# Head sums of an RWKV block: one fp32 product, or two fp32r products of a split operand

## The chip, the cores and the metric

The kernel runs on one core of a Trainium2 chip. The metric is the device time of one execution in microseconds (us); the median of several runs counts. A core has five engines that work in parallel, each with its own queue of instructions in fixed order: TensorE (in profiles PE, its weight loads PEld), VectorE (DVE), ScalarE (ACT), GpSimd (POOL) and SyncE (SP), which issues the transfers here. An instruction that needs another engine's result waits on a semaphore, and everything behind it in its queue waits with it.

## The reference

One residual block on x (1 x 1024 x 1024, float32): a norm, one large input projection, two branches side by side (stick-breaking attention with 8 heads of 64 channels, RWKV-7 time mixing with 8 heads of 64 channels), a gated merge with an output projection, and a SwiGLU feed-forward part. The change lies in the RWKV branch, cut here to what uses sums over a head's 64 channels:

```python
kk = (k * k_k).reshape(B, S, H, N)
kk = kk / jnp.maximum(jnp.linalg.norm(kk, axis=-1, keepdims=True), 1e-12)   # sum of squares over N
k = k * (1.0 + (a - 1.0) * k_a)
y = wkv7_scan(r_h, heads(decay), k_h, v_h, kk, heads(a))
mean = jnp.mean(y, axis=-1, keepdims=True)
var = jnp.mean(jnp.square(y - mean), axis=-1, keepdims=True)                # sum of squares over N
y = ((y - mean) * lax.rsqrt(var + GN_EPS)).reshape(B, S, RW_WIDTH) * lnx_w + lnx_b
bonus = (jnp.sum(r_h * k_h * r_k, axis=-1, keepdims=True) * v_h)            # sum over N
return ((y + bonus.reshape(B, S, RW_WIDTH)) * g)
```

## The kernel before

Activations lie with channels on the 128 partitions and tokens along the free axis. Two heads of 64 channels make a pair, and the RWKV branch has 4 pairs; each pair is worked in two halves of 512 tokens (`H`). One pair and one half is a unit, so there are 8 units. A sum over a head's channels is a sum over 64 partitions, made by TensorE: the left operand is `ones`, a 128 x 128 block matrix with a 64 x 64 block of ones for each head, and the right operand the 128 x 512 tile to be summed. The result has the sum on each of the head's 64 rows.

The large products run in fp32r, a form of fp32 that TensorE takes at another rate than plain fp32. To keep precision, an operand x is split into a high part (x cast to fp32r, on ScalarE) and a low part (x minus the high part, also fp32r, mostly on VectorE): the method `split`. Each k-step of a large product is then three fp32r products (high by high, high by low, low by high: `mm3`).

Work is recorded first and ordered afterwards. Each call such as `nc.tensor.matmul` becomes an `Op` with a price from the function `cost`, and `schedule` places the ops one by one on their engines by these prices, by priorities, and by when a tile's place comes free. Each engine then issues in that order, fixed when the kernel is built. So any new or cheaper operation can move others on all engines.

Stages, as the profile names them by tiles:

- `norm_in` and `lora`, up to some 90 us.
- The RWKV stage: `project` makes `k`, `r`, `v` of a pair (psum tiles `d`, rows `d_d<-big_h`), `rw_elementwise` prepares a unit, `rw_inverse` inverts small triangular blocks on VectorE (62 small dependent operations for a unit, tiles `q`, rows `q_q`), `rw_chain` carries the state through 8 chunks a unit (`c_c<-b_sv,b_nx`, then `c_c<-b_xv,b_bkt`; GpSimd scales the old state into `sp` meanwhile), and `rw_post` normalises. Gate projections (`gate_tiles`, also `d_d`) have a low priority and fill TensorE between.
- `attention`: per head products `e_e<-b_kst,...`, sigmoids on ScalarE (tile `nb`, behind a load of another table of functions, which waits for the last logarithm and exponential of `rw_post`), a scan on VectorE (`b_nb<-b_nb`), transposes (`c_c<-cst_cst,b_nb`), a split into `b_wt`, and products into `y`. The projections for the pairs to come (`d_d` again, with the splits `b_kst`, `b_ql`, `b_vhl`, `wlo`) run between.
- `merge`, `output`, `ffn`: large products.

Each unit makes three sums with `ones`: the squares of `k` (tile `t0` into `pn`, in front of everything that the inverse needs), `r * k * r_k` (tile `rk` into `pb`, for the bonus `bv`), and the squares of `y` in `rw_post` (tile `t0` into `pn`). That makes 24 products of 128 x 128 by 128 x 512 in plain fp32. SBUF tiles of class `b` share 27 places of 1040 columns; a plain fp32 tile of up to 520 columns takes half a place, other tiles a whole one.

Of the kernel before, what the change touches and what calls it, by code (L numbers as in the profile page):

```python
# [7 lines left out]
F32R = mybir.dt.float32r  # L8
BF16 = mybir.dt.bfloat16
AF = mybir.ActivationFunctionType  # L10
ALU = mybir.AluOpType
# [4 lines left out]
P = 128  # L16
# [3 lines left out]
H = 512  # L20
# [20 lines left out]
CC_ID, CC_CEN, CC_ONE, CC_MA, CC_DM, CC_TI, CC_SC, CC_N = 0, 128, 256, 384, 512, 640, 896, 1408  # L41
# [189 lines left out]
class Block:  # L231
# [325 lines left out]
    def proj(self, w, hf, cls="d"):  # L557
# [3 lines left out]
        self.mm3(ps, w, self.hT, KT, lambda x, k: x[:, k, :], lambda x, k: x[k // 4][:, k % 4, sl])  # L561
        return ps


    def rstd(self, srcs, junk):
        nc = self.nc
        ss = self.t("tiny", [P, 4])
        for i, s in enumerate(srcs):
            nc.scalar.activation(junk, s, AF.Square, accum_out=ss[:, i : i + 1])
        return self.rstd_of(ss, len(srcs))  # L570
# [20 lines left out]
def hybrid_block(tc, x, w_in, consts, params, rows, ups, gup, w_sb, w_rw, w_o, w_fg, w_fu, w_fd, out):  # L591
    b = Block(tc, {a.tensor.name for a in (x, w_in, consts, params, rows, ups, gup, w_sb, w_rw, w_o, w_fg, w_fu, w_fd)})
    nc = b
    T = b.t
    with ExitStack() as es:
        b.open(es)
        b.cls("cst", 1, CC_DM)
        b.cls("par", 1, PC_N)
        b.cls("small", 3, 16)
        b.cls("tiny", 4, 4)  # L600
        b.cls("ss", 8, 4)
        b.cls("carry", 5, 1)
        b.cls("pl", 3, 8)
        b.cls("bf", 2, P)
        b.cls("sp", 3, CH)
        b.cls("q", 4, 256)
        b.cls("big", 4, 4 * S)
        for n in ("raw", "whi", "wlo"):
            b.cls(n, 2, S)
        b.cls("b", NB, 1040, halves=True)  # L610
        for n, k in (("d", 2), ("e", 2), ("c", 2), ("y", 2)):
            b.cls(n, k, H, psum=True)

        cst, par = T("cst", [P, CC_DM]), T("par", [P, PC_N])
        b.xin = []
        for m in range(8):
            b.xin.append(T("b", [P, D], F32, "x"))
            nc.sync.dma_start(b.xin[m], x[m * P : m * P + P, :])
            if m == 0:
                nc.sync.dma_start(cst, consts[:, 0:CC_DM])  # L620
                b.gbc = T("b", [P, D])
                nc.sync.dma_start(b.gbc, rows[0:1, :].broadcast_to([P, D]))
            if m == 3:
                b.w_lora = [b.load(w_in[24], [P, KT, P])]
                nc.sync.dma_start(par, params)
            if m == 5:
                b.w_lora.append(b.load(w_in[25], [P, KT, P]))
        b.ident = cst[:, CC_ID : CC_ID + P]
        b.cen = cst[:, CC_CEN : CC_CEN + P]
        b.ones = cst[:, CC_ONE : CC_ONE + P]  # L630
        b.mask_a = cst[:, CC_MA : CC_MA + P]
        b.tinit = consts[:, CC_TI : CC_TI + 256]
        b.scanm = consts[:, CC_SC:CC_N]
        b.eps = T("small", [P, 2])
        nc.gpsimd.memset(b.eps[:, 0:1], RMS_EPS)
        nc.gpsimd.memset(b.eps[:, 1:2], GN_EPS)
        b.identb = T("bf", [P, P], BF16)
        nc.gpsimd.tensor_copy(b.identb, b.ident)
        b.dmask = T("bf", [P, P], BF16)
        dm = T("q", [P, P])  # L640
        nc.sync.dma_start(dm, consts[:, CC_DM : CC_DM + P])
        nc.gpsimd.tensor_copy(b.dmask, dm)
        b.om = T("small", [P, 14])
        nc.gpsimd.tensor_scalar(out=b.om, in0=par[:, PC_MU : PC_MU + 14], scalar1=-1.0, scalar2=1.0, op0=ALU.mult, op1=ALU.add)
        b.oka = T("small", [P, 4])
        nc.gpsimd.tensor_scalar(out=b.oka, in0=par[:, PC_KA : PC_KA + 4], scalar1=-1.0, scalar2=1.0, op0=ALU.mult, op1=ALU.add)
        b.pc = lambda col: par[:, col : col + 1]

        b.gsc = [b.scratch([P, S], f"gsc{j}") for j in range(16)]
        b.orw_d = [b.scratch([P, S], f"orw{p}") for p in range(PAIRS)]  # L650
        b.x2_d = b.scratch([S, D], "x2d")
        b.w_in, b.w_sb, b.w_rw = w_in, w_sb, w_rw
        b.ngate = 0

        b.steady = STEADY[0]
        norm_in(b)
        lora(b, ups, gup)
        b.steady = STEADY[1]
        rwkv(b)
        b.steady = STEADY[2]  # L660
        attention(b)
        b.steady = STEADY[3]
        merge(b)
        b.steady = True
        output(b, x, w_o, rows)
        ffn(b, w_fg, w_fu, w_fd, rows, out)
        b.issue()


def norm_in(b):  # L670
    nc = b.nc
    T = b.t
    b.hT = tuple([T("big", [P, 4, S], F32R, "h") for q in range(2)] for i in range(2))
    b.table("natural_log_exp_and_others")
    def scale(m):
        xs = T("b", [P, D], F32, "xs")
        return xs, b.rstd([b.xin[m]], xs)

    ahead = [scale(0), scale(1)]
    for m in range(8):  # L680
        xs, r = ahead.pop(0)
        nc.vector.scalar_tensor_tensor(out=xs, in0=b.xin[m], scalar=r, in1=b.gbc, op0=ALU.mult, op1=ALU.mult)
        if m + 2 < 8:
            ahead.append(scale(m + 2))
        b.to_channels(("e", "c"), xs, m, b.hT)
        if m in (2, 4):
            w = b.w_lora[m // 2 - 1]
            hi, lo = T("b", [P, KT, P], F32R), T("b", [P, KT, P], F32R)
            nc.scalar.copy(hi, w)
            nc.gpsimd.tensor_tensor(out=lo, in0=w, in1=hi, op=ALU.subtract)  # L690
            b.w_lora[m // 2 - 1] = hi, lo
# [91 lines left out]
def rwkv(b):  # L783
    T = b.t
    b.table("natural_log_exp_and_others")
    carry = {}
    units = [[{}, {}] for p in range(PAIRS)]

    def project(p):
        for name, j in (("k", 4 + p), ("r", p), ("v", 8 + p)):  # L790
            w = b.weights(b.w_in[12 + j], [P, KT, P])
            for hf in range(2):
                ps = b.proj(w, hf)
                units[p][hf][name] = T("b", [P, H], F32, name)
                shifted(b, ps, carry, j, hf, units[p][hf][name])

    project(0)
    for p in range(PAIRS):
        for hf in range(2):
            rw_elementwise(b, units[p][hf], p, hf, b.spill[p][hf])  # L800
        if p + 1 < PAIRS:
            with Offset(b, PROJ):
                project(p + 1)
        gate_tiles(b, GATES_R[p])
        with Offset(b, CHAIN):
            for hf in range(2):
                rw_chain(b, units[p], p, hf)
                with Offset(b, POST):
                    rw_post(b, units[p][hf], p, hf, b.spill[p][hf])


def rw_elementwise(b, u, p, hf, spill):
    nc = b.nc
    T = b.t
    pc, oka, cen, ones, mask_a, tinit = b.pc, b.oka, b.cen, b.ones, b.mask_a, b.tinit
    r, k, v = u["r"], u["k"], u["v"]
    lo, hi = slice(0, CH), slice(CH, P)
    halves = (lo, hi)
# [18 lines left out]

    t0 = T("b", [P, H], F32, "tmp")
    nc.scalar.activation(t0[:], k[:], AF.Square, scale=pc(PC_KK + p))
    pn = T("e", [P, H])  # L840
    nc.tensor.matmul(pn[:], lhsT=ones, rhs=t0[:], start=True, stop=True)
    rn = T("b", [P, H], F32, "tmp")
    nc.vector.tensor_scalar(out=rn[:], in0=pn[:], scalar1=1e-24, scalar2=None, op0=ALU.max)
    nc.scalar.activation(rn[:], rn[:], AF.Ln)
# [18 lines left out]

    rk = T("b", [P, H], F32, "tmp")
    nc.vector.scalar_tensor_tensor(out=rk[:], in0=r[:], scalar=pc(PC_RK + p), in1=kp[:], op0=ALU.mult, op1=ALU.mult)
    pb = T("e", [P, H])
    nc.tensor.matmul(pb[:], lhsT=ones, rhs=rk[:], start=True, stop=True)
    bv = T("b", [P, H], F32, "bv")
    nc.vector.tensor_tensor(out=bv[:], in0=v[:], in1=pb[:], op=ALU.mult)
    u["bv"] = bv  # L870
# [153 lines left out]
def rw_post(b, u, p, hf, spill):  # L1024
    nc = b.nc
    T = b.t
    pc, ones = b.pc, b.ones
    y, t0 = T("b", [P, H], F32, "ptmp"), T("b", [P, H], F32, "ptmp")
    nc.scalar.copy(y, u["y"])
    nc.scalar.activation(t0[:], y[:], AF.Square)  # L1030
    pn = T("c", [P, H])
    nc.tensor.matmul(pn[:], lhsT=ones, rhs=t0[:], start=True, stop=True)
    rs = T("b", [P, H], F32, "ptmp")
    nc.scalar.activation(rs[:], pn[:], AF.Ln, scale=1.0 / CH, bias=b.eps[:, 1:2])
    nc.scalar.activation(rs[:], rs[:], AF.Exp, scale=-0.5)
    nc.vector.scalar_tensor_tensor(out=rs[:], in0=y[:], scalar=pc(PC_LW + p), in1=rs[:], op0=ALU.mult, op1=ALU.mult)
    nc.vector.scalar_tensor_tensor(out=rs[:], in0=rs[:], scalar=pc(PC_LB + p), in1=u["bv"][:], op0=ALU.add, op1=ALU.add)
    g = T("b", [P, H], F32, "ptmp")
    nc.sync.dma_start(g[:], spill["g"][:])
    nc.gpsimd.tensor_tensor(out=rs[:], in0=rs[:], in1=g[:], op=ALU.mult)  # L1040
    nc.sync.dma_start(b.orw_d[p][:, hf * H : hf * H + H], rs[:])
# [534 lines left out]
```

## Time and profile before

| | |
|---|---|
| median of 3 runs | 1660.45 us (1658.56 to 1661.47) |
| the profiled execution | 1659.71 us, its span 1657.9 us |
| TensorE busy | 1603.0 us, 97% of the span |
| VectorE busy | 1124.1 us, 68% |
| ScalarE busy | 718.0 us, 43% |
| GpSimd busy | 206.6 us, 12% |
| mean granted TensorE clock | 0.998 |

The profile is one execution. Its rows name the source line (L528, where recorded operations are issued, for all of them, so one goes by tiles), engine, operation, output tile, input tiles and shape. Buffer numbers are left out, and a tile stands under the name of whichever allocation used its place last; so the sums with `ones` read `e_e<-b_cum,cst_cst` or `c_c<-b_tmp,cst_cst` and the like, with `cst` the constants that hold `ones`. One plain fp32 product is shown as two MATMUL instructions. "Idle before" is time in which the engine had nothing to do ahead of an instruction, with what ended it.

### The profile page before, as it was taken

To read this page: it belongs to the slowest core of one execution; us is meant where nothing else is said; L and a number is where in the kernel's file an instruction comes from. 1 tells how busy PE (TensorE), PEld (TensorE's weight loads), DVE (VectorE), ACT (ScalarE), POOL (GpSimd) and SP (SyncE) were. 2 spreads that over 40 slices of the span, in tenths; PEclk is the share of its full clock that TensorE was granted. 3 is DMA by queue.
4 is the path that set the end of the run, shared out by engine and by line. 5 is a ranking of instruction groups with operands and counts; after the bars stand their busy time and mean duration, and the time that the engine had idled before them with its cause. 6 is when DMAs were issued, how large, how long until landed. Compare 5 with 4: busy or idle time off the path is not lost.

```text
span 1657.9 us, 23575 instructions
## 1 busy us (share of the span) xinstructions
PE 1603.0 (97%) x8876; PEld 1273.8 (77%) x8876; DVE 1124.1 (68%) x1999; ACT 718.0 (43%) x1403; POOL 206.6 (12%) x344
## 2 busy tenths in 40 slices
PE   6999999999999999999999999999999999999998
PEld 5777776776777777777787788888888888888886
DVE  6567789668784877878248446766666666778484
ACT  7532334433334656566433434333233322455352
POOL 2021232512313010000015120000000000000000
PEclk9999999999999999999999999999999999999999
DMA  6533222242320000001644501233332332774455
GB/s 217 201 88 91 78 80 79 75 137 72 99 77 34 32 26 14 26 26 39 214 135 142 195 39 58 89 96 106 110 107 97 127 95 96 276 270 141 137 167 178
DMA packets 107108, 180.96 MB, mean 109 GB/s; under 512 B 42353, under 2 KB 43505, under 8 KB 106993
## 3 DMA queue, kind: packets, MB, share of 16 engines
q1 hardware_dynamic: 106992, 179.44, 33.1%
q8 instruction: 70, 1.15, 0.3%
q14 instruction: 46, 0.37, 0.1%
HBM read 129.86 MB, written 47.45 MB: 107 GB/s over the span
## 4 chain that ended last, share of the span: by engine, by line
PE 74%; DVE 17%; ACT 4%; issue 3%; DMA 2%; POOL 0%; SPq 0%; DVEq 0%; ACTq 0%; POOLq 0%
PE d_d L528 31%; PE e_e L528 17%; PE c_c L528 15%; PE y_y L528 10%; DVE q_q L528 6%; DVE b_nb L528 3%; ACT b_qst L528 1%; DVE b_wt L528 1%; DVE wlo_wlo L528 1%; DVE b_sv L528 1%; ACT whi_whi L528 1%; DVE b_nx L528 1%; ACT b_wt L528 1%; DVE b_kst L528 1%; DMA b_b<-rows 0%
## 5 line engine op out<-in xcount | busy, mean ns | idle before, releaser
L528 PE MATMUL d_d<-big_h,whi_whi 128*128 128x512 f32 x1280 | 431.5, 408 | 3.7 <-DVE b_kst L528 2.8
L528 PEld LDWEIGHTS d_d<-big_h,whi_whi 128*128 128x128 f32 x1280 | 234.7, 189 | 52.0 <-issue 6.3
L528 PE MATMUL d_d<-big_h,wlo_wlo 128*128 128x512 f32 x640 | 260.3, 407 | 0.0
L528 PEld LDWEIGHTS d_d<-big_h,wlo_wlo 128*128 128x128 f32 x640 | 120.7, 189 | 24.0 <-issue 1.9
L528 DVE TENSOR_TENSOR wlo_wlo<-raw_raw,whi_whi 128x1024 fp32r<-128x1024 f32 (+1 forms) x60 | 70.6, 1177 | 40.0 <-ACT whi_whi L528 38.6
L528 ACT CAST whi_whi<-raw_raw 128x1024 fp32r<-128x1024 f32 (+1 forms) x60 | 55.9, 933 | 92.5 <-PE d_d L528 82.5
L528 DVE TENSOR_TENSOR q_q<-b_nl,q_q 128x2 f32<-128x2 f32 (+30 forms) x248 | 85.6, 345 | 11.0 <-PE y_y L528 2.7
L528 DVE TENSOR_TENSOR_SCAN b_nb<-b_nb 128x128 f32<-128x128 f32 (+3 forms) x64 | 87.5, 1395 | 1.0
L528 POOL TENSOR_SCALAR sp_sp<-b_sv,pl_pl 64x64 f32<-64x64 f32 x120 | 58.1, 485 | 117.7 <-DVE b_sv L528 110.8
L528 DVE TENSOR_REDUCE q_q<-q_q 128x1 f32<-128x2 f32 (+30 forms) x248 | 62.1, 250 | 6.7
L528 PE MATMUL d_d<-b_wd,big_act 128*128 128x512 f32 x264 | 66.6, 395 | 0.0
L528 PE MATMUL e_e<-b_wd,big_act 128*128 128x512 f32 x264 | 66.6, 394 | 0.0
L528 ACT CAST b_wd<-b_wraw 128x512 fp32r<-128x512 f32 x71 | 42.2, 620 | 53.2 <-DVE b_wraw L528 22.7
L528 DVE TENSOR_TENSOR b_wd<-b_wraw,b_wd 128x512 fp32r<-128x512 f32 x71 | 46.7, 686 | 23.4 <-ACT b_wd L528 23.4
L528 PEld LDWEIGHTS d_d<-b_wd,big_act 128*128 128x128 f32 x264 | 49.6, 188 | 11.8
L528 PEld LDWEIGHTS e_e<-b_wd,big_act 128*128 128x128 f32 x264 | 49.6, 188 | 11.8
L528 PE MATMUL c_c<-cst_cst,b_nb 128*128 128x128 f32 x288 | 47.9, 280 | 9.2 <-DVE b_wt L528 4.5
L528 ACT COPY b_xv<-c_c 64x64 f32<-64x64 f32 x64 | 13.3, 208 | 92.1 <-DVE b_xv L528 46.6
L528 ACT CAST b_wt<-c_c 128x512 fp32r<-128x512 f32 (+2 forms) x96 | 43.9, 481 | 21.0 <-PE c_c L528 19.9
L528 DVE TENSOR_TENSOR b_wt<-c_c,b_wt 128x512 fp32r<-128x512 f32 (+2 forms) x96 | 50.0, 547 | 4.5 <-ACT b_wt L528 3.8
L528 PEld LDWEIGHTS c_c<-cst_cst,b_nb 128*128 128x128 f32 x288 | 32.6, 140 | 23.9 <-DVE b_wt L528 12.2
L528 PE MATMUL c_c<-b_wd,big_act 128*128 128x512 f32 x198 | 50.6, 395 | 0.0
(651 smaller groups left out, 3558.0 us busy)
## 6 DMA issues: line engine op xcount, KB each, us to landing
raw_raw<-w_in SPq DMA_DIRECT2D x42, 512.0 KB, 3.4
raw_raw<-w_fg SPq DMA_DIRECT2D x22, 512.0 KB, 3.5
raw_raw<-w_fu SPq DMA_DIRECT2D x22, 512.0 KB, 4.0
b_wraw<-w_fd SPq DMA_DIRECT2D x22, 512.0 KB, 5.0
act<-b_u SPq DMA_DIRECT2D x40, 256.0 KB, 3.4
b_x<-x SPq DMA_DIRECT2D x16, 512.0 KB, 6.3
raw_araw<-act SPq DMA_DIRECT2D x14, 512.0 KB, 4.3
whi_araw<-act SPq DMA_DIRECT2D x14, 512.0 KB, 4.9
```

Source lines behind the costliest of these rows:

```text
L528: getattr(getattr(self.real, op.engine), op.method)(**kw)
```

## The change

A new method `head_sums` splits the tile to be summed into a high part (cast to fp32r on ScalarE) and a low part (the difference, on GpSimd), both in one new tile `hs`, and sums them by two fp32r products into the same psum tile. It takes the place of the fp32 product at all three sites. `ones` becomes an fp32r tile of its own, cast once at the start.

```diff
+    def head_sums(self, cls, x):
+
+        nc = self.nc
+        both = self.t("b", [P, 2, H], F32R, "hs")
+        hi, lo = both[:, 0], both[:, 1]
+        nc.scalar.copy(hi, x)
+        nc.gpsimd.tensor_tensor(out=lo, in0=x, in1=hi, op=ALU.subtract)
+        ps = self.t(cls, [P, H])
+        nc.tensor.matmul(ps, lhsT=self.ones, rhs=hi, start=True, stop=False)
+        nc.tensor.matmul(ps, lhsT=self.ones, rhs=lo, start=False, stop=True)
+        return ps
...
+        b.cls("ones", 1, P)
...
-        b.ones = cst[:, CC_ONE : CC_ONE + P]
...
+        b.ones = T("ones", [P, P], F32R)
+        nc.scalar.copy(b.ones, cst[:, CC_ONE : CC_ONE + P])
...
     nc.scalar.activation(t0[:], k[:], AF.Square, scale=pc(PC_KK + p))
-    pn = T("e", [P, H])
-    nc.tensor.matmul(pn[:], lhsT=ones, rhs=t0[:], start=True, stop=True)
+    pn = b.head_sums("e", t0)
...
-    pb = T("e", [P, H])
-    nc.tensor.matmul(pb[:], lhsT=ones, rhs=rk[:], start=True, stop=True)
+    pb = b.head_sums("e", rk)
...
     nc.scalar.activation(t0[:], y[:], AF.Square)
-    pn = T("c", [P, H])
-    nc.tensor.matmul(pn[:], lhsT=ones, rhs=t0[:], start=True, stop=True)
+    pn = b.head_sums("c", t0)
```

The function `cost` prices the two forms differently, so the order of all engines changes. In the lists below a number behind a name is that of the allocation (it differs between the two builds), and `x2` at the end means two equal instructions in a row.

First place: TensorE at a sum in the first pair, among projections. Before:

```order
L528 MATMUL d_d_844<-big_h_186,wlo_wlo_753 128x512
L528 MATMUL e_e_874<-b_a_576,cst_cst_136 128x512
L528 MATMUL d_d_878<-big_h_169,whi_whi_811 128x512
L528 MATMUL d_d_878<-big_h_175,whi_whi_811 128x512
L528 MATMUL e_e_897<-cst_cst_136,b_sm_284 128x128 x4
```

After, at a sum of the same pair (`b_hs` holds the two parts):

```order
L528 MATMUL d_d_1007<-big_h_171,wlo_wlo_906 128x512
L528 MATMUL e_e_1014<-b_hs_1005,ones_ones_147 128x512
L528 MATMUL d_d_1007<-big_h_171,whi_whi_884 128x512
L528 MATMUL d_d_1007<-big_h_177,whi_whi_884 128x512
L528 MATMUL d_d_1007<-big_h_171,wlo_wlo_906 128x512
L528 MATMUL d_d_1007<-big_h_171,whi_whi_884 128x512
L528 MATMUL d_d_1007<-big_h_177,whi_whi_884 128x512
L528 MATMUL d_d_1007<-big_h_171,wlo_wlo_906 128x512
L528 MATMUL e_e_1014<-b_hs_1005,ones_ones_147 128x512
```

The one product has become two, and between the high and the low part six projection products stand here; at other sums the two follow each other.

Second place: GpSimd within a chain of the first pair, where it scales the state (`sp`) for each chunk. Before:

```order
L528 TENSOR_SCALAR sp_sp_1819<-b_sv_885,pl_pl_684 64x64 x2
L528 TENSOR_TENSOR b_ar_1863<-b_a_476 128x8x64
L528 TENSOR_SCALAR sp_sp_1875<-b_sv_1182,pl_pl_740 64x64 x2
L528 COPY pl_pl_1895<-b_a_476 128x8
L528 TENSOR_TENSOR b_v_1330<-b_v_1330,b_sh_427 128x512
```

After:

```order
L528 TENSOR_SCALAR sp_sp_1784<-b_sv_898,pl_pl_686 64x64 x2
L528 TENSOR_TENSOR b_hs_1787<-b_tmp_973,b_hs_1787 128x512
L528 MEMSET b_sv_1807 64x64 x2
L528 TENSOR_SCALAR sp_sp_1826<-b_sv_898,pl_pl_686 64x64 x2
L528 TENSOR_SCALAR sp_sp_1865<-b_sv_898,pl_pl_686 64x64 x2
```

A subtract of a sum now stands between the scalings of two chunks, as other operations of that size did here and there before.

Third place: TensorE in attention's first pair, from the second group of transposes of its fourth step to that step's first product into `y`. Before:

```order
L528 MATMUL c_c_5778<-cst_cst_136,b_nb_5693 128x128 x4
L528 MATMUL d_d_5720<-big_h_175,whi_whi_5402 128x512
L528 MATMUL d_d_5720<-big_h_169,wlo_wlo_5420 128x512
L528 MATMUL d_d_5720<-big_h_186,whi_whi_5402 128x512
L528 MATMUL d_d_5720<-big_h_195,whi_whi_5402 128x512
L528 MATMUL d_d_5720<-big_h_186,wlo_wlo_5420 128x512
L528 MATMUL d_d_5720<-big_h_186,whi_whi_5402 128x512
L528 MATMUL y_y_5794<-b_wt_5753,b_vhl_5506 128x128
```

After:

```order
L528 MATMUL c_c_5954<-cst_cst_136,b_nb_5878 128x128 x4
L528 LDWEIGHTS bf_bf_145
L528 MATMUL e_e_5951<-bf_bf_296,bf_bf_145 128x128
L528 MATMUL e_e_5951<-b_kst_4846,b_ql_5054 128x384
L528 MATMUL e_e_5966<-b_kst_4846,b_qst_5052 128x512
L528 LDWEIGHTS bf_bf_145
L528 MATMUL e_e_5966<-bf_bf_296,bf_bf_145 128x128
L528 MATMUL e_e_5966<-b_kst_4846,b_ql_5054 128x512
L528 MATMUL d_d_5942<-big_h_177,whi_whi_5581 128x512
L528 MATMUL d_d_5942<-big_h_171,wlo_wlo_5593 128x512
L528 MATMUL y_y_5981<-b_wt_5925,b_vhl_5662 128x128
```

Where six projection products stood, there are now two, and products of the next head: the projections have moved to earlier places in the queue.

More of the change, by code (lines that the diff above doesn't have):

```diff
@@ L814, in rw_elementwise @@
     T = b.t
-    pc, oka, cen, ones, mask_a, tinit = b.pc, b.oka, b.cen, b.ones, b.mask_a, b.tinit
+    pc, oka, cen, mask_a, tinit = b.pc, b.oka, b.cen, b.mask_a, b.tinit
     r, k, v = u["r"], u["k"], u["v"]
@@ L1026, in rw_post @@
     T = b.t
-    pc, ones = b.pc, b.ones
+    pc = b.pc
     y, t0 = T("b", [P, H], F32, "ptmp"), T("b", [P, H], F32, "ptmp")
```

## The prediction, made before the changed kernel was run

> **What bounds the kernel now.** I read the page's busy shares first, then its chain, then busy time by stage.
>
> ```profile
> PE 1603.0 (97%) x8876; PEld 1273.8 (77%) x8876; DVE 1124.1 (68%) x1999; ACT 718.0 (43%) x1403; POOL 206.6 (12%) x344
> PE 74%; DVE 17%; ACT 4%; issue 3%; DMA 2%; POOL 0%; SPq 0%; DVEq 0%; ACTq 0%; POOLq 0%
> core 0: us, PE busy (x) PEld busy (x) DVE busy (x) ACT busy (x) POOL busy (x), PEclk, DMA share, GB/s
> 90.00:533.00 443.00, 426.94 (x3390) 326.74 (x3390) 328.75 (x883) 172.42 (x369) 130.60 (x262) 1.00 0.29 84
> 533.00:600.00 67.00, 62.67 (x375) 49.21 (x374) 49.42 (x66) 43.01 (x94) 6.38 (x9) 1.00 0.08 28
> ```
>
> TensorE is busy 97% of the span and carries 74% of the chain that ended last. The fourth row is the RWKV stage, where 23 of the 24 changed products run: TensorE 426.94 of 443 us, at a granted clock of 1.00, VectorE 74%, ScalarE 39%, GpSimd 29%. The last row is the start of attention. TensorE's waits in the RWKV stage:
>
> ```profile
> PE y_y L528 <- DVE q_q L528: 3.0, 2, 1.7
> PE d_d L528 <- DVE b_kst L528: 2.8, 2, 2.0
> PE c_c L528 <- DVE b_xv L528: 2.0, 5, 0.8
> PE y_y L528 <- issue: 1.7, 2, 1.1
> PE c_c L528 <- ACT b_xv L528: 1.5, 4, 0.5
> ```
>
> These are small (16 us of idle in 443), because projections and gates (`d_d`) stand between all dependent steps. So TensorE's work counts, but only as long as enough such filler is left: the units' latency (elementwise, VectorE's inverse `q_q`, chain) runs beneath it.
>
> **The product itself.** TensorE's instructions around one of the 24, in order of time (start, length, count):
>
> ```profile
> 142.17 0.62 PE L528 MATMUL d_d<-big_h,whi_whi 128*128 128x512 f32 x2
> 142.63 0.40 PE L528 MATMUL d_d<-big_h,wlo_wlo 128*128 128x512 f32 x1
> 142.86 0.63 PE L528 MATMUL d_d<-big_h,whi_whi 128*128 128x512 f32 x2
> ...
> 144.25 1.02 PE L528 MATMUL e_e<-b_cum,cst_cst 128*128 128x512 f32 x2
> 144.71 1.02 PE L528 MATMUL d_d<-big_h,whi_whi 128*128 128x512 f32 x2
> 145.57 1.05 PE L528 MATMUL e_e<-cst_cst,b_a 128*128 128x128 f32 x8
> ```
>
> Lengths overlap, so I go by starts. Three fp32r products take 142.17 to 142.86, 0.23 us each. One fp32 product (two instructions, the old form) and two fp32r ones take 144.25 to 145.57, 1.32 us: 1.32 - 0.46 = 0.86 for the fp32 product. Two fp32r products cost 0.46, so each sum saves 0.40, and 24 of them 9.5 us of TensorE. This presumes that products with the fp32r ones run at the rate of the other fp32r products.
>
> **What is added.** 24 casts on ScalarE and 24 subtracts on GpSimd, priced by the nearest operations of the same size:
>
> ```profile
> L528 ACT CAST b_wd<-b_wraw 128x512 fp32r<-128x512 f32 x71 | 42.2, 620 | 53.2 <-DVE b_wraw L528 22.7 <-PE y_y L528 19.5 <-DMA b_wraw<-w_fd 9.9
> L528 POOL TENSOR_TENSOR b_tmp<-b_sh,b_tmp 128x512 f32<-128x512 f32 x2 | 2.6, 1290 | 2.4 <-DVE b_tmp L528 1.6 <-DVE q_q L528 0.8
> ```
>
> ScalarE gets 24 x 0.62 = 14.9 us on 172, GpSimd 24 x 1.29 = 31.0 on 131: neither becomes a bound. A sum's result comes 0.62 + 1.29 - 0.40 = 1.5 us later, handoffs aside. For the norm of `k` that stands in front of the unit's inverse: the order takes up the first unit's inverse behind 502 `d_d` products where it was 470, and what is left of such shifts at the stage's end is in the 3.0 us below, so it is no term of its own. For the bonus and after the chain little hangs on it except, in the last unit, the start of attention's sigmoids. Queued behind a subtract on GpSimd are the `sp` scalings of the chain (place two of the order): at worst 1.29 us, with the chain's own two products and a copy in between as cover. The cast of the ones costs nothing:
>
> ```profile
> 4.87 0.29 POOL L528 CAST bf_bf<-cst_cst 128x128 bf16<-128x128 f32 x1 [4.00 <-DMA cst_cst<-consts]
> 8.77 1.28 DVE L528 SCALAR_TENSOR_TENSOR b_xs<-b_x,tiny_tiny,b_b 128x1024 f32<-128x1024 f32 x1 [8.77 <-DMA b_b<-rows]
> ```
>
> The constants are there at 4.87, and the first scaled tile waits for another transfer until 8.77; if that cover went, the price is one small cast, some 0.3 us. The 24 `hs` tiles each hold one full place of the 27 in class `b`; the order shows projections moved earlier, not later, so I price that at nothing.
>
> **Where the saved time goes.** Counted in the order, 1435 `d_d` products stand ahead of attention's first transposes before, 1489 after: 54 more, 54 x 0.23 = 12.5 us of filler pulled forward. All 24 sums stand ahead of that point too. So TensorE reaches it 12.5 - 9.5 = 3.0 us later. The saving was not used to end the RWKV stage sooner; it must be earned in attention's first stretch, which has 12.5 us less filler. From order row 2350 of 5936 on, TensorE's order is the same, so what is gained by there shifts the rest. That stretch:
>
> ```profile
> 541.00:567.00 26.00, 23.80 (x137) 18.53 (x135) 22.72 (x31) 16.53 (x40) 3.29 (x4) 1.00 0.08 31
> 541.00:598.00 57.00, 53.19 (x302) 41.47 (x300) 43.55 (x60) 35.87 (x82) 6.38 (x9) 1.00 0.09 31
> L528 DVE TENSOR_TENSOR wlo_wlo<-raw_raw,whi_whi 128x1024 fp32r<-128x1024 f32 x12 | 14.7, 1226 | 12.3 <-ACT whi_whi L528 11.3 <-PE y_y L528 1.0
> L528 DVE TENSOR_TENSOR b_ql<-d_d,b_qst 64x512 fp32r<-64x512 f32 x15 | 10.3, 689 | 8.2 <-ACT b_qst L528 8.0 <-issue 0.3
> L528 DVE TENSOR_TENSOR b_kst<-d_d,b_kst 64x512 fp32r<-64x512 f32 x12 | 8.3, 689 | 3.5 <-ACT b_kst L528 3.4
> L528 DVE TENSOR_TENSOR b_vhl<-c_c,b_vhl 128x512 fp32r<-128x512 f32 x8 | 5.4, 680 | 3.6 <-ACT b_vhl L528 3.5
> ```
>
> TensorE's 53.19 us fall to 40.7. VectorE's fall less: one `wlo`, two `b_ql` and two `b_kst` leave the stretch and one `b_vhl` enters it, 1.23 + 4 x 0.69 - 0.68 = 3.3, so 43.55 becomes 40.3. The two engines now have equal work there, and each head goes TensorE, ScalarE, VectorE, TensorE, so they can't both be full. If TensorE keeps its idle of 3.8 us, the stretch takes 44.5 (-12.5); if VectorE runs as full as in its densest part (22.72 of 26, 87%), 40.3/0.87 = 46.3 (-10.7); if only as full as over the whole stretch now (76%), 52.7 (-4.3). I take 46.3: the new order is as dense throughout as the first 26 us are now.
>
> **GpSimd and VectorE.** An existing GpSimd operation of the subtract's kind, beside the inverse:
>
> ```profile
> 255.91 1.20 POOL L528 TENSOR_TENSOR b_ar<-b_sh,b_a 128x512 f32<-128x512 f32 x1
> 256.26 0.88 DVE L528 TENSOR_TENSOR q_q<-b_nl,q_q 128x12 f32<-128x12 f32 x1
> 257.37 0.18 DVE L528 TENSOR_TENSOR q_q<-b_nl,q_q 128x14 f32<-128x14 f32 x1
> ```
>
> VectorE's product takes 0.88 us where a larger one takes 0.18, and ends at 257.14, just after GpSimd's at 257.11: it was held 0.70 us. 24 new subtracts can thus cost VectorE between 0 and 24 x 0.70 = 16.8 us; what reaches TensorE is less. GpSimd has 32 operations of this kind in the stage now (four a unit), and TensorE waits 3.0 us for the inverse: 24/32 x 3.0 = 2.3, which I take, since that row is what such holds have cost so far.
>
> The Trainium skill (SBUF — State Buffer, "SBUF: two separate sides") says that a VectorE operation with two SBUF inputs and a GpSimd operation that reads SBUF take a shared port pair as an exclusive lock, and the loser blocks for the whole instruction. The trace agrees: the held product ended 0.03 us after GpSimd's. Taken at its worst, a whole subtract each, the rule would make the VectorE loss 24 x 1.29 = 31.0 us instead of 16.8.
>
> **The sum**, against the profiled execution's 1659.71 (span 1657.9): +3.0 - 10.7 + 2.3 = -5.4, so 1654.3. The median of the runs, 1660.45, stands 0.7 above that execution: 1655.0.
>
> **Rivals.**
> 1. All of the saving arrives: -12.5 in the stretch, no new holds, -9.5, 1650.9. For it: TensorE's 97%. Against it: VectorE would have to run at 40.3 of 44.5, 91%, for the whole stretch.
> 2. The saving is lost in attention: the stretch takes 52.7, 3.0 - 4.3 + 2.3 = +1.0, 1661.4. For it: 76% is what VectorE reaches over two heads. Against it: part of its idle time there was waiting for TensorE's filler, which is gone.
> 3. Slower: the subtracts hold VectorE inside the inverses, and products that stand fixed in TensorE's order wait for them. Without holds the sum is -7.7; each hold on the path adds 0.70, so from 16 of 24 on the kernel is slower by over 3.3 us: 1664.0, and 1669.6 with all 24. For it: the row with 0.88. Against it: TensorE now waits for the inverse twice in 16 times, and the inverses fill only part of the stage. The skill's lock is this rival's cause.
> 4. The products with fp32r ones are no cheaper: 24 x (2 x 0.86 - 0.86) = 20.6 us more than now, 1681. Against it: every fp32r row here runs at 0.23.
>
> **Chances.** Forecast 0.45 (its own range 1652 to 1657), all of the saving 0.13, lost in attention 0.25, slower by holds 0.14, not cheaper 0.03. A measurement of this kernel tells about 0.2%, 3.3 us, from no change. The first two cases are faster by more (0.58), the third is within it (0.25), the last two slower (0.17). The range, 1649.5 to 1664, holds the first three cases and the edge of the fourth.
>
> **What would show it.** The 24 sums as pairs of 0.23 us products in the profile after, TensorE's busy time down by about 9 us; its first transposes of attention some 3 us later than 542; from there to the place that was 598 before, 46 us instead of 57, with VectorE near 87%; more waits of `y_y` for `q_q`, and `q_q` products of up to 1.3 us. The prediction is wrong if TensorE's idle before the first transposes changes by more than 5 us (the reordered queue meets other waits than now), or if that stretch keeps its 57 us.

## The result, and the profile after

The changed kernel takes 1675.30 us (median of 5 runs, 1675.25 to 1677.25) against 1660.24 for the kernel before (5 runs; the 1660.45 above is the median of the first 3): a ratio of 1.0097, 95% interval 1.0085 to 1.0108. It is slower by 15 us where 5 us less was forecast. The profiled execution took 1675.28 us, its span 1673.5, 15.6 more than before.

The page's busy shares and its chain, after:

```profile
PE 1604.9 (96%) x8876; PEld 1283.0 (77%) x8876; DVE 1134.4 (68%) x1999; ACT 731.7 (44%) x1428; POOL 243.7 (15%) x368
PE 56%; DVE 5%; ACT 2%; issue 1%; DMA 1%; DVEq 0%; SPq 0%
```

TensorE's busy time did not fall by 9 us, it rose by 2. Was the product no cheaper? TensorE's instructions around one sum in the RWKV stage, after (start, length):

```profile
263.92 0.39 PE L528 MATMUL d_d<-big_h,whi_whi 128*128 128x512 f32 x1
264.14 0.39 PE L528 MATMUL c_c<-b_hs,ones_ones 128*128 128x512 f32 x1
264.37 0.39 PE L528 MATMUL d_d<-big_h,whi_whi 128*128 128x512 f32 x1
```

By starts a product with the fp32r ones takes 0.23 us, as forecast, so some 9.5 us of work did leave TensorE; what put as much back shows in the granted clock. Busy time by stage (columns as before: TensorE, its weight loads, VectorE, ScalarE, GpSimd, then the granted clock):

```profile
core 0: us, PE busy (x) PEld busy (x) DVE busy (x) ACT busy (x) POOL busy (x), PEclk, DMA share, GB/s
90.00:533.00 443.00, 411.42 (x3150) 320.02 (x3150) 330.57 (x853) 173.57 (x360) 151.14 (x261) 0.97 0.28 82
200.00:300.00 100.00, 85.67 (x727) 66.28 (x727) 81.85 (x222) 41.75 (x90) 34.85 (x68) 0.93 0.28 79
533.00:600.00 67.00, 64.04 (x535) 52.35 (x530) 45.32 (x81) 44.12 (x101) 18.75 (x31) 1.00 0.09 33
```

Two things are new in the RWKV stage: TensorE is idle for 31.6 us of 443 (16.1 before), and its granted clock is 0.97, in one stretch 0.93, where it was 1.00. Its waits there:

```profile
PE y_y L528 <- DVE q_q L528: 8.0, 3, 7.1
PE y_y L528 <- issue: 3.7, 1, 3.7
PE c_c L528 <- DVE b_xv L528: 3.7, 7, 1.0
PE d_d L528 <- ACT b_bv L528: 2.4, 1, 2.4
```

7.1 of the 8.0 us and all of the 3.7 are one place, the inverse of the third unit. Before, then after (the dots stand for more `d_d` products and two products of the chain):

```profile
272.26 0.69 PE L528 MATMUL y_y<-q_q,b_nx 32*32 32x32 f32 x32 [1.67 <-DVE q_q L528]
272.89 0.50 PE L528 MATMUL d_d<-big_h,whi_whi 128*128 128x512 f32 x1
...
277.63 0.40 PE L528 MATMUL d_d<-big_h,wlo_wlo 128*128 128x512 f32 x1
279.16 0.69 PE L528 MATMUL y_y<-q_q,q_q 32*32 32x32 f32 x32 [1.13 <-issue]
```

```profile
272.48 0.39 PE L528 MATMUL d_d<-big_h,wlo_wlo 128*128 128x512 f32 x1
279.99 1.06 PE L528 MATMUL y_y<-q_q,b_nx 32*32 32x32 f32 x32 [7.12 <-DVE q_q L528]
281.51 0.79 PE L528 MATMUL c_c<-b_sv,b_nx 128*128 128x128 f32 x2 [0.46 <-ACT b_nx L528]
286.02 1.06 PE L528 MATMUL y_y<-q_q,q_q 32*32 32x32 f32 x32 [3.72 <-issue]
```

In the order before, 20 `d_d` products stood between the first group that uses an inverse (`y_y<-q_q,b_nx`) and the second (`y_y<-q_q,q_q`) of that unit, behind 739 others. In the new order 768 stand ahead of the first group and none between: the filler on offer was used up. The first two units had taken it: 502 and 650 stand ahead of their first groups, where it was 470 and 603. At the fourth unit the two orders stand level again (803 against 804). At the other seven inverses 5 to 23 stand between the groups.

The span is cut best at attention's first transposes, the place up to which the forecast counted. Windows of before up to there and over attention's first stretch, then the same two of after:

```profile
90.00:542.04 452.04, 435.98 (x3453) 333.84 (x3452) 333.65 (x891) 178.72 (x380) 131.20 (x263) 1.00 0.29 82
542.04:598.00 55.96, 52.15 (x297) 40.70 (x295) 42.51 (x58) 35.58 (x80) 5.77 (x9) 1.00 0.09 32
```

```profile
90.00:572.39 482.39, 450.28 (x3509) 351.81 (x3508) 349.47 (x896) 196.53 (x410) 167.07 (x287) 0.97 0.27 78
572.40:613.60 41.20, 38.00 (x239) 30.35 (x237) 37.61 (x53) 30.97 (x73) 4.57 (x7) 1.00 0.10 33
```

The transposes come at 572.39 instead of 542.04, 30.35 us later: idle time rose from 16.06 to 32.11 (+16.05) and busy time by 14.30, where 54 more products less the saving make 3.0. Of the other 11.3, the lower clock accounts for 9.8 at most (worked out further down), and the rest was not traced. The rest of the span fell from 1115.86 to 1101.1 (-14.8). The balance, +30.35 - 14.8, is the +15.6.

### The profile page after: what moved, and what is told of

It reads as the page before. It is cut to its first block, busy times and chain, and to the rows that moved or that the text cites. A ratio compares the mean times of both kernels' runs of the same rounds, so it can differ in the third digit from the quotient of the medians.

```text
span 1673.5 us, 23674 instructions
## 1 busy us (share of the span) xinstructions
PE 1604.9 (96%) x8876; PEld 1283.0 (77%) x8876; DVE 1134.4 (68%) x1999; ACT 731.7 (44%) x1428; POOL 243.7 (15%) x368
## 4 chain that ended last, share of the span: by engine, by line
PE 56%; DVE 5%; ACT 2%; issue 1%; DMA 1%; DVEq 0%; SPq 0%
PE d_d L528 19%; PE e_e L528 15%; PE c_c L528 13%; PE y_y L528 8%; DVE b_nb L528 3%; DVE b_wt L528 1%; ACT b_qst L528 0%; ACT b_wt L528 0%; ACT whi_whi L528 0%; ACT b_nb L528 0%; DVE b_wol L528 0%; DMA raw_raw<-w_o 0%; DMA b_g<-gsc 0%; ACT q_q L528 0%; DVE b_ql L528 0%
## 5 line engine op out<-in xcount | busy, mean ns | idle before, releaser
L528 PEld LDWEIGHTS d_d<-big_h,whi_whi 128*128 128x128 f32 x1280 | 238.6, 190 | 50.6 <-ACT b_bv L528 2.8
L528 DVE TENSOR_TENSOR q_q<-b_nl,q_q 128x2 f32<-128x2 f32 (+30 forms) x248 | 93.4, 377 | 18.8 <-PE y_y L528 10.2
```

Source lines behind the costliest of these rows:

```text
L528: getattr(getattr(self.real, op.engine), op.method)(**kw)
```

## The experiments

Each diff is cut to its main lines and is against the changed kernel unless another is named. The kernels of e1, e5, e9 and e15 leave the low part out of the sums, so their results differ from the reference; they serve for timing alone. Line numbers in the rows shift with the edits; all are the line where recorded operations are issued. "Ahead" below is the number of `d_d` products that the order puts ahead of attention's first transposes. A held product is one of the inverses' 248 VectorE products that took over 0.2 us more than the fastest of its shape, counted in VectorE's rows of each profile: 7 before (5.0 us over in all), 18 after (13.7 us).

**e1: after's order without the subtracts.**

```diff
-        nc.gpsimd.tensor_tensor(out=lo, in0=x, in1=hi, op=ALU.subtract)   # left out when issued
-        nc.tensor.matmul(ps, lhsT=self.ones, rhs=lo, start=False, stop=True)
+        nc.tensor.matmul(ps, lhsT=self.ones, rhs=hi, start=False, stop=True)
```

> The changed kernel in its own order, instruction for instruction, without the 24 subtracts on GpSimd: the second product of each sum takes the high part again. The low part is left out, and the sums come out doubled; TensorE's work is unchanged. Theory F (the order ran out of filler products ahead of the third unit's inverse, and TensorE's gap there halves its clock): the order is the same, so the gap of several us at 273 to 288 stays, TensorE's idle time in 90 to 533 stays above 25 us (31.6 in the changed kernel, 16 before), and the time stays at 1669 to 1677 us. Theory H (subtracts on GpSimd hold VectorE inside the inverses, rival 3): 24 holds of 0.70 us are gone from VectorE, the idle time falls to some 16 us, and the time to 1652 to 1662.

1662.87 us, ratio to before 1.0019 (1.0011 to 1.0028). The time fell by 12.4 us, nearly as H (holds) said, 0.9 above its range; and yet the gap stayed as F (filler) said:

```profile
276.38 1.06 PE L533 MATMUL y_y<-q_q,b_nx 32*32 32x32 f32 x32 [6.56 <-DVE q_q L533]
277.91 0.80 PE L533 MATMUL c_c<-b_sv,b_nx 128*128 128x128 f32 x2 [0.46 <-ACT b_nx L533]
282.42 1.06 PE L533 MATMUL y_y<-q_q,q_q 32*32 32x32 f32 x32 [3.71 <-issue]
```

VectorE's busy time fell by 8.3 us to 1126.1, held products from 18 to 12 (13.7 to 9.2 us over), so about half of the 8.3 us lies in the inverses' products. Attention's first transposes come at 560.28 instead of 572.39: TensorE's idle time ahead of them fell from 32.11 to 24.38, and its clock was halved in two stretches there instead of four. Both theories hold a part.

**e5 and e9: is it the hold, the wait for the low part, or GpSimd's queue?** e5 keeps all subtracts, with nobody waiting for them; e9 has GpSimd write for as long instead.

```diff
 e5
-        nc.tensor.matmul(ps, lhsT=self.ones, rhs=lo, start=False, stop=True)
+        nc.tensor.matmul(ps, lhsT=self.ones, rhs=hi, start=False, stop=True)
 e9, besides
-        nc.gpsimd.tensor_tensor(out=lo, in0=x, in1=hi, op=ALU.subtract)
+        for part in (lo, lo, lo[:, 0 : H // 2]):
+            nc.gpsimd.memset(part.bitcast(F32), 0.0)
```

> The changed kernel in its own order, with all 24 subtracts on GpSimd, but each sum's second product takes the high part again, so that nothing waits for a low part (it is left out of the sums, which come out doubled). Leaving the subtracts out altogether (e1) took 12.4 us off. Theory H (they hold VectorE): VectorE's busy time stays near 1134 us, the time at 1671 to 1677. Theory L (the sums wait for the low part): as without subtracts, 1661 to 1666.

> As e5 (the order of the changed kernel, the second product takes the high part again), but in place of each subtract GpSimd clears the low part three times (128x512, 128x512 and 128x256, estimated at 0.52, 0.52 and 0.27 us from the row of 950 ns for a memset of 64x1024): GpSimd is occupied for as long as by a subtract, but reads nothing from SBUF. With the subtracts the time was 1673.5 (e5), without them 1662.9 (e1). Theory H (VectorE is held by what GpSimd's subtract reads): VectorE's busy time falls to 1126 us and the time to 1661 to 1666. Theory O (GpSimd's own queue is what is late, above all the scalings of the state): 1670 to 1676.

e5 took 1673.46 us (ratio 1.0085, 1.0071 to 1.0098), e9 1663.77 (1.0021, 1.0012 to 1.0031). GpSimd's groups in e9:

```profile
L528 POOL MEMSET b_hs<- 128x512 f32 x48 | 25.3, 526 | 1.9
L528 POOL MEMSET b_hs<- 128x256 f32 x24 | 7.5, 312 | 1.4
```

GpSimd's busy time is nearly that of the changed kernel (241.8 us against 243.7), VectorE's is 10.0 us less (1124.4). So waiting for the low part is worth 1.8 us and GpSimd's occupation 0.9 (e9 against e1), both no more than the intervals allow for noise, and its reading beside VectorE the rest: about 10. Held products are 18 in e5 and 11 in e9. Rows of the changed kernel show one hold:

```profile
263.76 1.56 POOL L528 TENSOR_TENSOR b_hs<-b_ptmp,b_hs 128x512 fp32r<-128x512 f32 x1 [7.96 <-issue]
264.60 0.75 DVE L528 TENSOR_TENSOR q_q<-b_nl,q_q 128x2 f32<-128x2 f32 x1
265.57 0.16 DVE L528 TENSOR_TENSOR q_q<-b_nl,q_q 128x3 f32<-128x3 f32 x1
```

VectorE's product of 2 columns takes 0.75 us beside the subtract and ends at 265.35, just after it (265.32); the next, of 3, takes 0.16. Of the 11 additional held products, 6 go with the subtracts (18 to 12). The other 5 are left in e1: operations that GpSimd had before now stand beside an inverse, by the new order, as in these rows of the changed kernel:

```profile
342.91 1.27 POOL L528 TENSOR_TENSOR b_tmp<-b_ptmp,b_tmp 128x512 f32<-128x512 f32 x1 [4.44 <-DVE b_tmp L528]
342.93 1.28 DVE L528 TENSOR_TENSOR q_q<-b_nl,q_q 128x14 f32<-128x14 f32 x1
```

**e4 and e8: the subtract on VectorE,** with an order planned for it (e4), and in after's order (e8).

```diff
-        nc.gpsimd.tensor_tensor(out=lo, in0=x, in1=hi, op=ALU.subtract)
+        nc.vector.tensor_tensor(out=lo, in0=x, in1=hi, op=ALU.subtract)
```

> The changed kernel with the subtract on VectorE instead of GpSimd (24 x 0.68 = 16.3 us more on VectorE, 31 less on GpSimd). Its order keeps filler at all inverses (20 products or more inside the third unit's). Theory F: idle time below 20 us, clock 1.00, 1648 to 1662 us. Theory H: the holds are gone, 1650 to 1660 as well. Theory L: latency little changed, 1665 to 1675. If VectorE's added work decides instead, above 1675.

> The changed kernel in its own order, with each subtract carried out by VectorE at the place in the program where GpSimd had it: VectorE has 24 x 0.68 = 16.3 us more to do and GpSimd holds it 24 times less. e4 has the subtract on VectorE too, but an order of its own with filler at every inverse. If e4's gain came from the missing holds, 1653 to 1662 here too. If it came from its order, the gap at the third unit's inverse stays here, and the time is 1662 to 1672.

e4 took 1653.37 us, ratio 0.9959 (0.9946 to 0.9971): faster than both kernels. e8 took 1672.82 (1.0081, 1.0068 to 1.0095), just above what was expected. VectorE's own 16 us in after's order cost nearly what the holds cost, so e4's gain comes with its order: 1525 ahead, 21 products between the third unit's two groups, and TensorE at full clock in the stretch that had 85.67 at 0.93:

```profile
200.00:300.00 100.00, 95.14 (x796) 73.65 (x797) 83.95 (x225) 44.53 (x94) 32.48 (x71) 1.00 0.31 87
```

**e3, e10 and e15: filler at the third unit.** e3 moves a gate projection there; e10 does so in the kernel before; e15 is e3 with e1's edit.

```diff
-GATES_R = (4, 0, 2, 6)
+GATES_R = (4, 1, 1, 6)
```

> The changed kernel with one of 12 gate projections of the RWKV stage moved from the third pair to the second: 48 more filler products are on offer at the third unit's inverse; up to there the order is that of the changed kernel. Theory F: no gap over 3 us around 273 to 288, granted clock 1.00 there, idle time in 90 to 533 below 22 us, 1653 to 1665 us. Theory H and theory L: subtracts, casts and the order ahead of the place are the same, 1670 to 1678.

> The kernel before, with the gate projection moved from the third pair to the second as in e3. Theory F (e3 cured the gap that the changed order had): the kernel before has filler at the third unit's inverse anyway, so nothing is gained, 1657 to 1664 us. Rival: the gate's place is better whatever the sums do, 1648 to 1656, and e3's gain of 19 us says nothing on the change.

> e3 (gate moved, filler at every inverse) without the subtracts, as e1 (the second product takes the high part again). Without the gate's move the subtracts cost 12.4 us. If filler at the inverses covers the holds of VectorE, the subtracts cost little here: 1652 to 1657 us (e3 had 1656.0). If holds cost the same in any order, 1643 to 1647.

e3 took 1656.01 us, ratio 0.9976 (0.9968 to 0.9985), 19.3 us less than the changed kernel. At the same place:

```profile
279.83 0.63 PE L528 MATMUL d_d<-big_h,whi_whi 128*128 128x512 f32 x2
280.39 0.69 PE L528 MATMUL y_y<-q_q,b_nx 32*32 32x32 f32 x32
281.01 0.50 PE L528 MATMUL d_d<-big_h,wlo_wlo 128*128 128x512 f32 x1
...
285.97 0.39 PE L528 MATMUL d_d<-big_h,wlo_wlo 128*128 128x512 f32 x1
286.66 0.69 PE L528 MATMUL y_y<-q_q,q_q 32*32 32x32 f32 x32 [0.30 <-PE d_d L528]
```

The inverse is not earlier (280.39 against 279.99, 286.66 against 286.02). TensorE has work until it comes, and that work need not be done later. The move changes the order behind that place too: 1546 products stand ahead. e10 took 1667.10 us, ratio 1.0036 (1.0024 to 1.0049), slower than before and beyond what either reading expected: the gate's place is no gain in itself, it serves the changed order. In e10's profile (of an execution of 1669.06 us) 30 products fewer than before stand ahead of the transposes, which still come 3.5 us later (545.52), with 17.1 us at half clock on the way, and the rest of the span is 5.9 us longer. e15 took 1650.73 (0.9941, 0.9928 to 0.9953), between its two expectations: with filler the subtracts cost 5.3 us (e3 less e15), not 12.4. Held products are 14 in e3 and 7 in e15, a difference of 7 as between after and e1 (6), so the holds are as many; filler covers about half of what they cost.

**e11 and e12: both cures, and another spread.**

```diff
 e11: e4, and
-GATES_R = (4, 0, 2, 6)
+GATES_R = (4, 1, 1, 6)
 e12: e4, and
+GATES_R = (4, 2, 2, 4)
```

> The changed kernel with both cures: subtract on VectorE (e4, 1653.4) and the gate moved (e3, 1656.0). If both cure the same loss (TensorE idle at the inverses), the second adds nothing: 1650 to 1657. If the losses by holds (10 to 12 us) and by missing filler are separate, 1640 to 1648.

> The subtract on VectorE (e4), and the gates of the pairs spread as 4, 2, 2, 4 instead of 4, 0, 2, 6. Its order has no place without filler at an inverse up to the fifth unit. If e4 still lost time to thin filler in the second pair, 1645 to 1651; if not, 1651 to 1656.

e11 1659.40 (0.9994, 0.9985 to 1.0003), e12 1655.04 (0.9970, 0.9958 to 0.9981). e11 missed both expectations and is worse than either cure alone. e12 lies where nothing was left to gain from another spread. No gain adds up here. Against e4, e11's transposes come 8.2 us later (564.52 against 556.36) and the rest of the span is as long; 2.6 us of the 8.2 are idle time, and TensorE's clock was halved for 10.2 us there, where e4's never was. What makes e11's waits longer was not found.

**e2, e13, e6, e16: operations and orders apart.** e2 and e13 keep all new operations and plan the pair of products at the fp32 product's price, e2 with cast and subtract at nothing besides. e6 has after's order with fp32 products of a copy, without subtracts. e16 is the kernel before, its product planned at the price of the pair.

```diff
 e2: self.price = 0.0 for copy and subtract, and as e13
 e13
+        self.price = 2 * H / 1.2 / 2
         nc.tensor.matmul(ps, lhsT=self.ones, rhs=hi, start=True, stop=False)
         nc.tensor.matmul(ps, lhsT=self.ones, rhs=lo, start=False, stop=True)
+        self.price = None
 e6, when issued: copy to fp32, subtract and first product left out
+        nc.tensor.matmul(ps, lhsT=self.ones32, rhs=hi.bitcast(F32), start=True, stop=True)
 e16, at the three products with ones of the kernel before
+    b.price = 2 * H / 2.4
```

> All operations of the changed kernel, but the order is planned as if a sum's two products cost together what the fp32 product did, and the cast and subtract nothing. In this order 20 to 24 filler products stand again inside the third unit's inverse, where the changed kernel has none. Theory F: TensorE's idle time in 90 to 533 falls below 20 us with the granted clock at 1.00, and the time to 1650 to 1662 us. Theory H: the same 24 subtracts are there, 1668 to 1678. Theory L (a sum's result comes later by cast and subtract, and the units are late by that whatever the order): 1665 to 1675.

> All operations of the changed kernel with GpSimd's subtracts; the order is planned with true prices for cast and subtract (e2 had them at nothing, and TensorE waited 12.5 us for parts not yet there), and with the fp32 product's price for the pair of products. 20 filler products stand inside the third unit's inverse. If filler at the inverses covers the holds of VectorE (10.6 us in the changed order, by e5 against e1), the time is 1653 to 1661 us. If the holds cost what they cost in any order that isn't made of e3's extra filler, 1662 to 1669. If it is 1672 or more, filler at that place is not what matters.

> The old fp32 products (of a copy of the tile) in the order of the changed kernel, instruction for instruction: no subtract, no second product, the fp32 product at the second one's place. What the order alone costs. Theory F: the gap ahead of the third unit's inverse products and the halved clock behind it stay, as in e1 where it was 6.6 us; TensorE has 24 x 0.40 = 9.6 us more to do than there, most of it no longer hidden: 1664 to 1673 us. Rival: the order costs only because TensorE comes to the gap early; nine sums stand ahead of it, 3.6 us, so the gap shrinks to 3 us and the time is that of the kernel before, 1658 to 1663.

> The kernel before with its fp32 products, ordered as if a sum's product cost what the pair costs now (427 ns instead of 853): another order, no other operation, 19 filler products inside the third unit's inverse. If the order costs by missing filler at that place alone, 1657 to 1662 us. If any other order than the one before can lose several us by where GpSimd's present operations and TensorE's waits fall (e10 lost 7, e6 9), 1664 to 1672, and the lost part of e1 and e13 needs no cause in the sums themselves.

e2 took 1675.62 us (1.0091, 1.0076 to 1.0107). That is where H had it, but the waits show that it tells nothing between F and H:

```profile
PE c_c L529 <- POOL b_hs L529: 7.9, 6, 2.8
PE e_e L529 <- POOL b_hs L529: 4.6, 6, 1.3
```

12.5 us of waits for a low part that the planner took to cost nothing. e13 corrects that and took 1667.47 (1.0044, 1.0030 to 1.0058), with 16 held products and 20 filler products inside the third unit's inverse. That lies where its expectation had holds that filler does not cover, so filler at this one place is not enough; that the holds are what it loses by was not tested, since no run leaves the subtracts out of its order, and its trace also has 3.1 us of waits for a low part. e6 took 1668.94 (1.0060, 1.0047 to 1.0073): after's order costs 9.5 us with no subtract at all. e16 took 1660.32 (1.0006, 0.9997 to 1.0015): another order, with filler at that place, costs nothing.

**e7 and e14: the halved clock.** Products that are overwritten fill TensorE's gaps at the third unit; e7 fills both (48 and 24), e14 the first (56).

```diff
+            for _ in range(56):   # ahead of the first product into ph of the third unit
+                nc.tensor.matmul(ph, lhsT=b.ones, rhs=b.hT[0][0][:, 0, 0:256], start=True, stop=True)
```

> The changed kernel, with 48 and 24 additional products of 128x256 (some 0.115 us each) that are overwritten, ahead of the two groups of the third unit's inverse products, where TensorE was idle for 7.1 and 3.7 us. Theory (the clock is halved because TensorE was idle): the granted clock stays at 1.00 from 277 to 291, the products there run in half the time, and the time falls by 2 to 4 us, 1671 to 1673.5. If the halving has another cause, the clock is halved there still, and the time is 1675 to 1677. Should the added products end too late, 1676 to 1680.

> As e7, but only the first gap is filled (56 products of 128x256, 6.8 us by e7's 5.84 us for 48), since e7's second group waited for its psum tile until 286.36 and then held up TensorE by 4.8 us. The clock stays at 1.00 until past 281; the idle 4 us before the second group of inverse products halves it again after that. So the price of the first gap's halved clock is measured alone: 1 to 3 us faster than the changed kernel, 1672 to 1674.5. If idle TensorE doesn't set the clock: 1675 to 1677.

e7 took 1678.27 (1.0114, 1.0100 to 1.0128), its second group being late because the added products ahead of it waited for its psum tile. e14 took 1675.03 (1.0087, 1.0073 to 1.0101), the time of the changed kernel, where 1 to 3 us less were expected:

```profile
273.31 6.78 PE L529 MATMUL y_y<-big_h,ones_ones 128*128 128x256 f32 x56
280.46 0.69 PE L533 MATMUL y_y<-q_q,b_nx 32*32 32x32 f32 x32 [0.37 <-DVE q_q L533]
281.82 0.49 PE L533 MATMUL c_c<-b_sv,b_nx 128*128 128x128 f32 x2 [0.66 <-ACT b_nx L533]
286.60 1.07 PE L533 MATMUL y_y<-q_q,q_q 32*32 32x32 f32 x32 [4.30 <-issue]
```

The clock followed TensorE's idle time, as expected: the first group takes 0.69 us where it took 1.06, the second, behind the idle 4.30, still 1.07. But what was won at the first group is waited away ahead of the second, so the halved clock of the first gap is worth nothing here.

## Why the prediction was wrong

- **The product's price** was right: 0.23 us each, 9.5 us of TensorE. In e4, whose clock was halved only at the very end, TensorE's busy time is 7.8 us below that of the kernel before (1595.2 against 1603.0).
- **The first term of the sum, the transposes 3.0 us later, is the step that failed.** It took the RWKV stage to be bound by TensorE's work, so that only the count of products mattered. They came 30.35 us later. The text had said that the work counts "only as long as enough such filler is left", and then counted filler ahead of one place at the stage's end instead of at each inverse. By the third unit's inverse none was left, since the first two units had taken more than before (650 ahead of the second inverse instead of 603). The 54 products that come from attention do not help there: the order places them behind the fourth unit, up to which both orders have issued as many.
- **Idle time unchanged** was its silent half, named among what would make the prediction wrong (more than 5 us): it went from 16.06 to 32.11. The halved clock follows from that. The four stretches at half clock hold 6.52, 3.41, 3.41 and 6.18 us of TensorE's busy time, 19.5, of which half, an estimate of 9.8, is the most that the clock can have cost; by e14 nothing was lost on the path in the first.
- **GpSimd's holds** were priced at 2.3 us between 0 and 16.8. They were worth about 10 in this order (e5 against e9) and, with the wait for the low part, 5.3 in e3's. The figure came from TensorE's waits for the inverse before, when filler covered them: it priced the holds and the cover together, and the cover went.
- **Attention's stretch**, 46.3 us forecast, took 41.2 (from 55.96), VectorE 37.61 of it, 91%. That is the density which rival 1 asked for and which I had thought too high. The 14.8 us won there are more than the 12.5 of that rival. The time from the transposes to the end fell by 0.25 to 0.27 us for each product pulled ahead of them (after 14.8 for 54, e3 29.2 for 111, e4 22.7 for 90), against 0.23 that each costs at its new place if nothing waits there, so pulling filler forward pays, by little, where the waits ahead still have enough of it.
- **Rival 3**, slower by holds, had the sign and half of the mechanism. Its holds were too many (24 of 0.70, where only 6 of the inverses' held products go with the subtracts), and its end, 1669.6, was still passed because it had no missing filler. The Trainium skill (SBUF — State Buffer, "SBUF: two separate sides") names GpSimd operations that read SBUF as the ones that lock the port pair against VectorE's two-input operations; e9 agrees, since memsets for as long took the cost away. **Rival 1** had 1650.9: e15, with filler and without subtracts, took 1650.73. So the whole saving can arrive, but the match of the figures is luck: e15's transposes come 18.8 us later than before, not 3.0, and the rest is 28.8 us shorter, not 12.5.
- **The `hs` places at nothing** were not tried apart. The new price alone did not make the order run out (e16 has 19 filler products at that place), nor did the places and the added operations at the old price (e13 has 20), nor all of it with the subtract on VectorE (e4 has 21). Which of them together did is open. So is what makes the waits in e10 and e11 longer, and what e13 loses; e2 shows only that an order is bad when it is planned with false prices.

Without holds the forecast's sum was 1652.7; e1 has 1662.9. So the 20 us between forecast and result are 12.4 of subtracts, against 2.3 priced, and 10 of the order. That the order's 10 are missing filler is argued from the idle time at the third unit and on e3 and e15, which fill it; both also move products elsewhere.

## What to carry to other kernels

An engine that is 97% busy because low-priority work fills its waits may give nothing back when its work gets less, as here, if the new order leaves a wait without filler: count filler between the instruction that waits and the one before it, wait by wait, not in sum. Before an elementwise operation goes to GpSimd, look whether VectorE runs a chain of small dependent operations beside it; here 0.68 us on VectorE with an order planned for it beat 1.3 us on GpSimd (1653.4 against 1675.3). But that too depends on the order: with the gate moved, GpSimd was the better place (e3's 1656.0 against e11's 1659.4). When a planner sets the order, an edit's own price and its order's price are measured apart by building one with the other's order.

## What the hardware showed

TensorE's granted clock fell to half four times in the changed kernel between 90 us and attention's first transposes, in steps of 3.41 us: for 13.65, 3.41, 3.41 and 6.83 us. It did not take an idle window. The 3.41 us ahead of each fall:

```profile
274.50:277.91 3.41, 0.00 (x0) 0.00 (x0) 3.20 (x9) 1.03 (x2) 1.44 (x2) 1.00 0.29 52
353.01:356.42 3.41, 1.87 (x16) 1.28 (x16) 3.24 (x9) 3.04 (x5) 0.75 (x3) 1.00 0.33 125
428.10:431.51 3.41, 1.55 (x17) 1.21 (x16) 2.38 (x4) 1.32 (x2) 1.17 (x1) 1.00 0.32 96
496.37:499.78 3.41, 1.43 (x5) 0.86 (x5) 3.29 (x7) 1.86 (x3) 0.00 (x0) 1.00 0.39 58
```

TensorE was busy for 0 to 55% of them. The longest single wait in the last of them was 2.4 us (`d_d` for `b_bv`, in the rows above). All four start on one grid of 3.41 us (23, 22 and 20 steps apart); of the windows of that grid from 90 to 565 that had full clock themselves, all with over 2.2 us busy were followed by full clock; of the six with less, these four were followed by half clock and two, with 1.79 us each, were not. So there is no sharp limit in these figures. The Trainium skill (TensorE: Matmul & The Clock Gate, "What's actually happening") gives a free-running window of 3413 ns, with which the steps agree, and the half clock after an idle window, where three of these rows show it after windows that were 42 to 55% busy.
